# One core: a list scheduler's table counts occupancy and latency of ScalarE and VectorE apart, and the first left operand of the last stage takes another buffer

## Chip, core and metric

The kernel runs on one core of a Trainium2 chip. The metric is the device time of one execution in microseconds (us), lower is better. Engines: TensorE (PE), VectorE (DVE), ScalarE (ACT), GpSimd (POOL) and SyncE (SP), whose queue issues all DMA transfers.

## What is computed

One layer of a hybrid encoder for two groups of rows: a prompt of 1024 frames, and a sample of 32 frames with a cache of 512 keys. The width is 1024, with 8 heads of 64 in each of two attention kinds, all in float32:

```python
qa, ka, va, ga, qb, kb, vb, gb = split(rmsnorm(h, g_pre) @ w_in)       # 1024 -> 8 x 512
oa = band_attention(qa, ka, va, rel_bias)      # own chunk of 64 frames and the 8 before, softmax
ob = stick_breaking(qb, kb, vb)                # w = exp(log_sigmoid(z) + sum of log_sigmoid(-z) of later keys)
y  = concat([oa * silu(ga), ob * silu(gb)]) @ w_out
h  = h + rmsnorm(y, g_post)
h  = h + sigmoid(h @ w_ple_gate) * (p @ w_ple)
```

The outputs are h of both groups and their keys and values.

## The kernel before

**Numbers.** Each float32 product is made of rounded parts: an operand x is split into hi (x rounded) and lo (x less hi), and a product is hi·hi + hi·lo + lo·hi on TensorE. So nearly every operand costs a cast on ScalarE and a subtraction on VectorE or GpSimd before TensorE can use it.

**Stages.** (1) To about 60 us: x is loaded, normalized and transposed. (2) To about 606 us: eight pairs of heads in the order A0, B0, A1, B1, A2, B2, A3, B3, where A is band attention and B stick-breaking. While one pair's attention runs, the projections of the next are computed: mm_q, mm_k, mm_v and mm_g, for each pair in three pieces of 352 columns, of which the name's last number tells (mm_kB2_0 is the first piece of the keys of pair B2). Their banks are two in turn ("mm"). A pair has two heads (SA11 are scores of pair A1, head 1), and a head eight blocks of 128 rows (SB10_3 is block 3 of pair B1, head 0). Scores go through three banks in turn ("S"). Band attention: scores SA, bias and maximum on VectorE (om, statA), exponential on ScalarE with the row's sum (be, sumsA), transposed weights on TensorE (ptwA) or through memory (swapA), split into wTh and wTl, and the product with the values PVA. Stick-breaking: scores SB, exponentials and a scan along the keys (om), weights be, then ptwB or swapB, wTh, wTl and PVB. (3) To 619 us: the products p @ w_ple (ple). (4) To 801 us: the output projection and then the gate, each by a scheme of seven block products in place of eight (P1, P2, P6, P7, P4, P5, P3, in this order). There are four sets of them: two for the output projection (o), two for the gate (g). o0P1 is product P1 of row tile 0; its left operand is A11o0, its right one oB11. P2 has A12o0 and oB21.

**What sets the order.** No order is written out. The kernel is told to a Recorder (L264) in program order; each operation becomes a node with what it must wait for. `Recorder.cost` (L338) gives two numbers for each: `busy`, how long it holds its engine, and `late`, how much later its result is there. `Recorder.order` (L372) plays the nodes through engine by engine: of those ready on the engine that is free first it takes the one with the smallest key (a class, then the program order), and so makes one sequence, by which the instructions then stand on each engine. A user on another engine is ready SEM = 60 ns after the result, one on TensorE another MARGIN = 400 ns later (L432). A DMA counts 1500 ns, its bytes at a rate, and 2000 ns of reserve (L419). Function table loads of ScalarE, which the chip needs when it goes from band attention's exponential to stick-breaking's functions and back, are not in the table; they are put in afterwards. All instructions are emitted at one line of `Recorder.emit`, L450, so the profile tells them apart by their tiles.

**The last stage's first operands.** The right operands oB11, oB21, oT3 and oT2 are split from weights that are staged in eight tiles, woB11_0, woT3_0 and so on to woT3_3 (L1454; each holds a slice of 128 rows of two operands). They go through a ring of two buffers with the tag "ao" in pool fb. The left operands of row tile 0 use the same ring behind them, or a buffer of its own with the same tag in pool fa: `Side.room` (L1539) puts every third one there. The row tile's products come in the order A11, A12, S2, S3, A22, S1, S4, and `taken` counts them. A buffer of the ring is free once the one that had it two tiles before has been read to the end.

Of the kernel before, what the change touches and what calls it, by code (L numbers as in the profile page):

```python
# [8 lines left out]
F32 = mybir.dt.float32  # L9
# [254 lines left out]
class Recorder:  # L264
# [72 lines left out]
    @staticmethod  # L337
    def cost(eng, method, args, kw, writes, reads):  # L338

        out = writes[0] if writes else None  # L340
        n = out.free() if isinstance(out, View) else 1
        psum = any(isinstance(v, (View, Segments)) and v.buf.psum for v in reads)
        if eng == "PE":
            if method == "transpose":
                return (109 if args[1].shape[0] > 64 else 62), 165
            return max(109.0, 2.5 + 0.449 * args[2].free()) * (1 if args[2].buf.dtype == F32R else 4), 165
        if eng == "ACT":
            return (165 if psum else 200) + 0.83 * n + (190 if "accum_out" in kw else 0), 0
        if eng == "DVE":
            if method == "tensor_tensor_scan":  # L350
                return 155 + 2.08 * n, 0
            if method == "tensor_copy" and not psum:
                return 155 + 0.53 * n, 0
            if method == "scalar_tensor_tensor":
                return 210 + 1.04 * n, 0
            return 155 + 1.04 * n + (83 if method == "tensor_tensor_reduce" else 0), 0
        if eng == "POOL":
            if method == "tensor_tensor":
                if n == 1:
                    return 400, 0  # L360
                return 190 + (1.77 if out.buf.dtype == F32 else 2.15) * n, 0
            if method == "tensor_scalar":
                return 255 + 0.86 * n, 0
            return 100 + 0.82 * n, 0
        size, run = 4, 0
        for v in (out, args[1]):
            if isinstance(v, View) and v.buf.pool is not None:
                size, run = 4 * v.shape[0] * v.free(), 4 * v.shape[-1]
        return ISSUE, max(size / DMA_RATE, size / run * (8.5 + 0.0365 * run) / 16)


    def order(self):  # L372
# [10 lines left out]
        free = dict.fromkeys(names, 0.0)  # L383
# [6 lines left out]
        while len(out) < len(self.ops):  # L390
            best = None
            for e in names:
                if now[e]:
                    t = free[e]
                elif soon[e]:
                    t = max(free[e], soon[e][0][0])
                else:
                    continue
                if best is None or t < best[0]:
                    best = (t, e)  # L400
            t, e = best
# [12 lines left out]
            o.at = t  # L414
            if e == "CTL":
                done = t
            elif e == "SP":
                free[e] = t + o.busy
                line = max(line, t + o.busy + DMA_NS) + o.late  # L419
                done = line + DMA_MARGIN  # L420
            else:
                if o.shared:
                    t = max(t, port - (DVE_SET if e == "DVE" else POOL_SET))
                    port = t + o.busy
                free[e] = t + o.busy
# [30 lines left out]
def stream_step(  # L456
# [756 lines left out]
    done = set()  # L1213
# [309 lines left out]
    class Side:  # L1523
# [343 lines left out]
```

## Time and profile before

| | us |
|---|---|
| median of 3 runs | 806.38 (805.48 to 808.88) |
| the profiled execution | 808.3 |
| its span, first to last instruction | 806.5 |
| TensorE busy | 784.5 |
| VectorE busy | 575.5 |
| ScalarE busy | 507.8 |
| GpSimd busy | 436.8 |
| mean granted TensorE clock | 0.996 of full speed |

The profile is of one execution. A row of the timeline gives start, duration, engine, line, operation, out<-in with the tiles' names (numbers left out) and the count of instructions in the row, and in brackets the idle time of the engine just before, with what ended it. A row of waits gives the waiting engine and its tile, what it waited for, and the sum, count and longest in us. A row of windows gives the stretch and, for PE, PEld, DVE, ACT and POOL, busy us and instructions, then the granted clock, the DMA share and GB/s. All times are us from the span's start.

### The profile page before, as it was taken

The page shows a single profiled execution, that of the slowest core. Times are in us where ns is not written, and L with a number is a line of the kernel's source. Part 1 is how long each engine was busy: PE and PEld are TensorE (multiplying, and loading weights), DVE is VectorE, ACT ScalarE, POOL GpSimd, SP SyncE. Part 2 cuts the span into 40 slices and gives each one's busy share as a digit, 9 for nine tenths or more (in the row PEclk, how much of TensorE's full clock was granted, in tenths as well). Part 3 has the DMA queues.
Part 4 walks back from the last instruction along what each step waited for, and adds up shares of the span by engine and source line. Part 5 has one row for each costly group of instructions (what it writes and reads, how often), then busy time and mean ns, then how long its engine had stood idle before and what let it go on. Part 6 is the DMA issues. An engine that isn't in the chain of part 4 may idle for free.

```text
span 806.5 us, 14268 instructions
## 1 busy us (share of the span) xinstructions
PE 784.5 (97%) x4646; PEld 722.4 (90%) x4646; DVE 575.5 (71%) x1007; ACT 507.8 (63%) x1063; POOL 436.8 (54%) x503
## 2 busy tenths in 40 slices
PE   8999999999999999999999999999998999999997
PEld 6899989999889998999999989999996877888786
DVE  6627678886588897778896878766355687586565
ACT  5636675676476655785666685543337867876741
POOL 5613656873556676234660336777541537699523
PEclk9999999999999999999999999999999999999999
DMA  8419987668877749745545667774579767659743
GB/s 275 152 38 276 232 247 243 168 181 237 229 210 228 203 147 272 190 137 152 125 115 159 153 171 231 218 211 151 156 236 329 245 188 231 216 179 343 249 137 131
DMA packets 160971, 161.08 MB, mean 200 GB/s; under 512 B 39153, under 2 KB 120793, under 8 KB 160898
## 3 DMA queue, kind: packets, MB, share of 16 engines
q1 hardware_dynamic: 160898, 160.18, 67.0%
q8 instruction: 37, 0.61, 0.3%
q14 instruction: 36, 0.29, 0.1%
HBM read 99.23 MB, written 52.49 MB: 188 GB/s over the span
## 4 chain that ended last, share of the span: by engine, by line
PE 84%; ACT 5%; POOL 3%; DVE 3%; DMA 2%; issue 2%; SPq 1%; DVEq 0%; ACTq 0%; POOLq 0%
PE mm_gB L450 6%; PE mm_gA L450 6%; PE mm_qA L450 5%; PE mm_kA L450 5%; PE mm_vA L450 5%; PE mm_qB L450 4%; PE mm_kB L450 4%; PE SB L450 4%; PE PVB L450 4%; PE mm_vB L450 3%; PE PVA L450 3%; PE SA L450 3%; PE ptwB L450 3%; PE o0P L450 3%; PE o1P L450 2%; PE g0P L450 2%
## 5 line engine op out<-in xcount | busy, mean ns | idle before, releaser
L450 DVE TENSOR_TENSOR_SCAN om<-om,SB 128x384 f32<-128x384 f32 (+5 forms) x96 | 95.6, 1005 | 12.1 <-ACT om L450 9.8
L450 POOL TENSOR_TENSOR be<-om 128x128 f32<-128x128 f32 (+7 forms) x64 | 77.5, 1216 | 49.4 <-DVE om L450 23.1
L450 ACT ACTIVATE om<-SB 128x384 f32<-128x384 f32 (+5 forms) x96 | 44.9, 494 | 29.9 <-DVE SB L450 17.7
L450 ACT ACTIVATE be<-om,statA 128x640 f32<-128x640 f32 (+3 forms) x64 | 44.5, 696 | 12.1 <-DVE statA L450 6.9
L450 ACT CAST wTh<-ptwB 128x512 fp32r<-128x512 f32 (+3 forms) x64 | 29.4, 482 | 21.1 <-PE ptwB L450 16.2
L450 DVE TENSOR_TENSOR wTl<-be,wTh 128x640 fp32r<-128x640 f32 (+1 forms) x32 | 35.5, 1108 | 7.1 <-ACT wTh L450 6.8
L450 DVE TENSOR_TENSOR wTl<-ptwB,wTh 128x512 fp32r<-128x512 f32 (+3 forms) x64 | 33.5, 545 | 7.7 <-ACT wTh L450 4.6
L450 DVE TENSOR_TENSOR wTl<-ptwA,wTh 128x512 fp32r<-128x512 f32 (+2 forms) x64 | 29.8, 482 | 11.6 <-ACT wTh L450 10.1
L450 PE MATMUL SB<-kdB,LB 128*128 128x384 f32 (+5 forms) x96 | 33.7, 354 | 1.9 <-DVE om L450 1.9
L450 DVE CUSTOM_DVE_ANT_0 om<-SA,biasA 128x320 f32<-128x320 f32 (+3 forms) x64 | 30.0, 483 | 6.2 <-PE SA L450 5.8
L450 PE MATMUL SB<-klB,LB 128*128 128x384 f32 (+5 forms) x96 | 32.9, 347 | 0.0
L450 DVE STREAM_TRANSPOSE om<-be 128x640 f32<-128x640 f32 (+1 forms) x32 | 28.8, 900 | 4.7 <-ACT be L450 2.3
L450 ACT CAST wTh<-ptwA 128x512 fp32r<-128x512 f32 (+2 forms) x64 | 26.1, 424 | 9.0 <-PE ptwA L450 8.2
L450 PE MATMUL SA<-kdA,LA 128*128 128x320 f32 (+2 forms) x96 | 30.0, 322 | 1.3 <-DVE LA L450 0.7
L450 POOL TENSOR_TENSOR sggA<-sggA,oggA 128x352 f32<-128x352 f32 x24 | 23.9, 997 | 13.6 <-DVE sggA L450 10.2
L450 POOL TENSOR_TENSOR oB<-oB,oB 128x256 f32<-128x256 f32 x32 | 24.4, 783 | 12.0 <-DMA oB<-in_w_out_dram 5.8
L450 PE MATMUL SA<-klA,LA 128*128 128x320 f32 (+2 forms) x96 | 29.3, 316 | 0.0
L450 PE MATMUL ptwB<-ident,be 128*128 128x128 f32 x192 | 29.3, 273 | 0.0
L450 ACT CAST wTh<-be 128x640 fp32r<-128x640 f32 (+1 forms) x32 | 24.9, 779 | 6.4 <-DMA be<-swapA 3.8
L450 PE MATMUL ptwA<-ident,be 128*128 128x128 f32 x160 | 26.8, 274 | 2.0 <-ACT be L450 1.3
L450 POOL TENSOR_TENSOR gB<-gB,gB 128x256 f32<-128x256 f32 x32 | 24.3, 783 | 4.7 <-DMA gB<-in_w_ple_gate_dram 4.3
L450 DVE TENSOR_TENSOR SB<-SB,maskb 128x128 f32<-128x128 f32 x64 | 17.6, 290 | 11.3 <-PE SB L450 11.1
(707 smaller groups left out, 2659.7 us busy)
## 6 DMA issues: line engine op xcount, KB each, us to landing
swapA<-om SPq DMA_DIRECT2D x16, 320.0 KB, 2.7
be<-swapA SPq DMA_DIRECT2D x64, 80.0 KB, 3.2
oB<-in_w_out_dram SPq DMA_DIRECT2D x16, 256.0 KB, 4.6
sum_dro<-oB SPq DMA_DIRECT2D x16, 256.0 KB, 3.8
gB<-in_w_ple_gate_dram SPq DMA_DIRECT2D x16, 256.0 KB, 4.2
sum_drg<-gB SPq DMA_DIRECT2D x16, 256.0 KB, 3.0
x<-in_x_prompt_dram SPq DMA_DIRECT2D x16, 256.0 KB, 4.0
h_dr<-h SPq DMA_DIRECT2D x8, 512.0 KB, 3.2
```

Of the source, the lines that this page charges most:

```text
L450: getattr(getattr(tc.nc, o.what[0]), o.what[1])(*args, **kw)
```

## The change

It changes the table of `Recorder.cost`, the moment from which a user on the same engine counts as ready in `Recorder.order`, and one number in `Side.room`. ScalarE's entries move 105 ns from `busy` to `late`, VectorE's 85 (150 for a multiplication with a row sum), and GpSimd's two-input operations get 40 ns of `late`, with 20 less of `busy` (a single column 400 to 535). A user on the same engine counts as ready when the result is there, not when the engine is free; on TensorE this stays as it was.

```diff
         if eng == "ACT":
-            return (165 if psum else 200) + 0.83 * n + (190 if "accum_out" in kw else 0), 0
+            return (60 if psum else 95) + 0.83 * n + (190 if "accum_out" in kw else 0), 105
         if eng == "DVE":
             if method == "tensor_tensor_scan":
-                return 155 + 2.08 * n, 0
+                return 120 + 2.1 * n, 85
...
-            return 155 + 1.04 * n + (83 if method == "tensor_tensor_reduce" else 0), 0
+            if method == "tensor_tensor_reduce":
+                return 90 + 1.04 * n, 150
+            return 70 + 1.04 * n, 85
         if eng == "POOL":
             if method == "tensor_tensor":
                 if n == 1:
-                    return 400, 0
-                return 190 + (1.77 if out.buf.dtype == F32 else 2.15) * n, 0
+                    return 535, 40
+                return 170 + (1.77 if out.buf.dtype == F32 else 2.15) * n, 40
...
             for u in users[id(o)]:
                 if u.eng == e and e != "SP":
-                    r = t if e == "CTL" else free[e]
+                    r = t if e == "CTL" else free[e] if e == "PE" else done
...
             if self.pair == 0:
-                one = Side.taken % 3 == 2
+                one = Side.taken % 3 == 0
```

The rows of all engines change their order. Three places on ScalarE follow. In the rows, numbers behind the underscore at a name's end are of no matter, and the line is L450 before and L452 of the change.

**Pair A1 to pair B1.** Before, from the first stick-breaking exponential (SB10_0) on. be with sumsA11 is the exponential of band attention, om from SB10 the one of stick-breaking:

```order
L450 ACT_TABLE_LOAD
L450 ACTIVATE om_165<-SB10_0_0_2887 128x128
L450 COPY stvB1_2564<-mm_vB1_1_2700 128x352
L450 ACT_TABLE_LOAD
L450 ACTIVATE be_179,sumsA11_1473<-om_165,statA11_7_2775 128x640
L450 COPY otA11_0_2811<-PVA11_0_2995 64x512
L450 CAST wTh_530<-ptwA11_5_0_2988 128x512
L450 CAST wh_kA2_0_2687<-wr_kA2_0_2961 128x512
L450 COPY sumrowA11_2904<-ptsA11_2949 8x128
L450 CAST wh_kA2_1_2693<-wr_kA2_1_2964 128x512
L450 ACT_TABLE_LOAD
L450 ACTIVATE om_165<-SB10_1_0_3005 128x256
```

Of the change, the same place:

```order
L452 ACTIVATE be_179,sumsA11_1435<-om_165,statA11_6_2752 128x640
L452 ACTIVATE be_179,sumsA11_1435<-om_165,statA11_5_2524 128x640
L452 COPY be_179<-PVsA0_2838 32x64 x2
L452 ACTIVATE be_179,sumsA11_1435<-om_165,statA11_7_2753 128x640
L452 CAST wTh_552<-ptwA11_5_0_2942 128x512
L452 ACT_TABLE_LOAD
L452 ACTIVATE om_165<-SB10_0_0_2881 128x128
L452 ACTIVATE om_165<-SB10_1_0_2958 128x256
L452 COPY otA11_0_2814<-PVA11_0_2996 64x512
L452 COPY sumrowA11_2910<-ptsA11_2915 8x128
```

The band exponential with statA11_7 has moved ahead of SB10_0, the copies and casts for the next projections behind SB10_3, and one table load stands where there were three.

**Pair B1 to pair A2.** Before. stvA2 from mm_vA2_2 is the copy that empties a projection's bank; kdA21, LA21, wh_kB2 and wh_qB2 are casts of operands:

```order
L450 CAST kdA21_3847<-stkA2_2922 64x1024
L450 CAST wh_kB2_0_3592<-wr_kB2_0_3786 128x512
L450 CAST LA21_3852<-stqA2_2976 64x1024
L450 CAST wh_kB2_1_3610<-wr_kB2_1_3789 128x512
L450 ACTIVATE om_165<-SB11_7_0_3753 128x512
L450 ACTIVATE om_165<-SB11_7_1_3835 128x512
L450 ACT_TABLE_LOAD
L450 ACTIVATE be_179,sumsA20_2506<-om_165,statA20_0_2777 128x128
L450 COPY stvA2_3343<-mm_vA2_2_3726 128x352
```

Of the change:

```order
L452 CAST wh_kB2_0_3579<-wr_kB2_0_3774 128x512
L452 CAST wh_kB2_1_3585<-wr_kB2_1_3776 128x512
L452 COPY stvA2_3364<-mm_vA2_2_3728 128x352
L452 CAST kdA21_3889<-stkA2_2928 64x1024
L452 CAST LA21_3898<-stqA2_2978 64x1024
L452 ACTIVATE om_165<-SB11_7_1_3876 128x512
L452 ACT_TABLE_LOAD
L452 ACTIVATE be_179,sumsA20_2519<-om_165,statA20_0_2784 128x128
L452 CAST wh_qB2_0_3870<-wr_qB2_0_3777 128x512
```

The copy of mm_vA2_2 has moved ahead of kdA21, LA21, the exponential of SB11_7_1, the table load and the exponential of A20.

**Into the output projection.** Before. A11o0 and A12o0 are the casts of the first left operands, xA11o0 and xA12o0 their copies, uo0 their source, ple the results of stage 3:

```order
L450 COPY xA11o1_7626<-uo1_7540 128x512
L450 CAST whA11o1_7392<-uo1_7540 128x512
L450 CAST oB11_7359<-woB11_3_7598 128x512
L450 CAST oB21_7360<-woB11_3_7598 128x512
L450 COPY ple8_0_7677<-ple8_0_7634 32x512
L450 CAST A11o0_7683<-uo0_6367 128x512
L450 CAST oT3_7362<-woT3_3_7623 128x512
L450 COPY xA12o0_7694<-uo0_6367 128x512
L450 CAST oT2_7361<-woT3_3_7623 128x512
L450 COPY ple8_1_7702<-ple8_1_7645 32x512
L450 CAST S2o0_7531<-s2_0_7668 128x512
L450 CAST A12o0_7715<-uo0_6367 128x512
```

Of the change, first where A11o0 stands now:

```order
L452 CAST oT3_7360<-woT3_1_7441 128x512
L452 CAST oT2_7359<-woT3_1_7441 128x512
L452 ACTIVATE sggB3_2_7472<-mm_gB3_2_7450 128x352
L452 CAST A11o0_7527<-uo0_6402 128x512
L452 CAST php6_7498<-ptp6_7266 128x512
L452 COPY g_post1_7549<-GP_7356 128x512
L452 COPY ple4_0_7281<-ple4_0_6868 128x512
L452 COPY xA11o0_7562<-uo0_6402 128x512
L452 COPY ple4_1_7282<-ple4_1_6877 128x512
L452 CAST oB11_7357<-woB11_2_7515 128x512
```

and, behind these, where A12o0 stands:

```order
L452 COPY ple7_1_7642<-ple7_1_7625 128x512
L452 COPY ple8_0_7664<-ple8_0_7637 32x512
L452 CAST oB11_7357<-woB11_3_7608 128x512
L452 CAST oB21_7358<-woB11_3_7608 128x512
L452 COPY ple8_1_7697<-ple8_1_7648 32x512
L452 CAST A12o0_7702<-uo0_6402 128x512
L452 CAST oT3_7360<-woT3_3_7629 128x512
L452 CAST oT2_7359<-woT3_3_7629 128x512
L452 COPY p1o0_7675<-o0P1_7661 128x512
L452 CAST S3o0_7707<-uo0_6402 128x512
```

A11o0 has moved from behind both casts of woB11_3 to ahead of both casts of woB11_2, and A12o0 now stands just behind those of woB11_3. On TensorE o0P1 with its twelve matmuls is followed by o0P2 with twelve, then o1P1; before, two of o0P1 and two of o1P1 came first, then the other ten, the rest of o1P1 and o0P2.

More of the change, by code (lines that the diff above doesn't have):

```diff
@@ L347, in cost @@
         if eng == "ACT":
-            return (165 if psum else 200) + 0.83 * n + (190 if "accum_out" in kw else 0), 0
+            return (60 if psum else 95) + 0.83 * n + (190 if "accum_out" in kw else 0), 105
         if eng == "DVE":
             if method == "tensor_tensor_scan":
-                return 155 + 2.08 * n, 0
+                return 120 + 2.1 * n, 85
             if method == "tensor_copy" and not psum:
-                return 155 + 0.53 * n, 0
+                return 70 + 0.53 * n, 85
             if method == "scalar_tensor_tensor":
-                return 210 + 1.04 * n, 0
-            return 155 + 1.04 * n + (83 if method == "tensor_tensor_reduce" else 0), 0
+                return 125 + 1.04 * n, 85
+            if method == "tensor_tensor_reduce":
+                return 90 + 1.04 * n, 150
+            return 70 + 1.04 * n, 85
         if eng == "POOL":
```

## The prediction

> **What bounds the kernel now.** I read the busy times first, then the chain of work that ended last, then what TensorE waited for, and only then single places.
>
> ```profile
> PE 784.5 (97%) x4646; PEld 722.4 (90%) x4646; DVE 575.5 (71%) x1007; ACT 507.8 (63%) x1063; POOL 436.8 (54%) x503
> PE 84%; ACT 5%; POOL 3%; DVE 3%; DMA 2%; issue 2%; SPq 1%; DVEq 0%; ACTq 0%; POOLq 0%
> ```
>
> TensorE is busy 784.5 of 806.5 us, and no matmul is added or removed. So the change can win no more than the 22 us in which TensorE stands still, plus matmuls that run slower than they need. ScalarE and VectorE have a third of their time free: a table that makes them look faster gains nothing by itself. It acts only through the order, where TensorE waits. Those waits, with total, count and longest:
>
> ```profile
> PE o0P L450 <- ACT A11o L450: 2.5, 1, 2.5
> PE ptx L450 <- DVE be L450: 2.2, 2, 1.3
> PE SB L450 <- DVE om L450: 1.9, 3, 1.1
> PE mm_kB L450 <- ACT stvA L450: 1.5, 1, 1.5
> PE PVA L450 <- ACT wTh L450: 1.3, 1, 1.3
> PE ptwA L450 <- ACT be L450: 1.3, 1, 1.3
> ...
> PE ptsA L450 <- DVE sumsA L450: 1.0, 2, 0.9
> PE SA L450 <- DVE LA L450: 0.7, 1, 0.7
> ...
> PE SA L450 <- DVE statA L450: 0.6, 1, 0.6
> PE ptwA L450 <- DVE wTl L450: 0.4, 2, 0.2
> ...
> PE ptwA L450 <- ACT ktB L450: 0.3, 1, 0.3
> PE PVsA L450 <- DVE otA L450: 0.2, 1, 0.2
> PE ptkB L450 <- ACT sumrowA L450: 0.2, 1, 0.2
> ```
>
> Three groups: the start (ptx), one wait where the output projection begins (o0P), and 15 small ones in attention. These 15 are the rows from SB to ptkB without o0P and ptx: 1.9+1.5+1.3+1.3+1.0+0.7+0.6+0.4+0.3+0.2+0.2 = 9.4 us, a mean of 0.63 us.
>
> **Does the new table fit the chip?** It says that a 128x512 instruction of ScalarE holds the engine about 100 ns less than it takes, and one of VectorE 85 ns less.
>
> ```profile
> 600.38 0.62 ACT L450 CAST oB<-woB 128x512 fp32r<-128x512 f32 x1
> 609.26 1.14 ACT L450 CAST oB<-woB 128x512 fp32r<-128x512 f32 x2
> 601.13 0.68 DVE L450 TENSOR_TENSOR oB<-woB,oB 128x512 fp32r<-128x512 f32 x1
> 619.91 1.28 DVE L450 TENSOR_TENSOR oB<-woB,oB 128x512 fp32r<-128x512 f32 x2
> ```
>
> One cast takes 0.62, two take 1.14: the second begins 0.52 after the first (1.14−0.62), 100 ns before that one ends. The new entry is 95+0.83·512 = 520 ns held and 105 more until the result is there; the old one was 625 held. For VectorE it is 1.28−0.68 = 0.60 against a new entry of 70+1.04·512 = 602, where the old one held 687. So the planner's idea of both engines was pessimistic by 12 to 16% (85 of 687, 100 of 625) for each queued instruction, and its new one is right. What is planned as ready 0.4 us ahead (MARGIN) will be so more exactly; but what the old table gave away as reserve is used up too. That is why I expect waits to go and others to come.
>
> The Trainium skill speaks against it: "VectorE: DVE Perf Modes", section "The DRAIN you can't avoid", has it that the next VectorE operation does not start until the pipe is empty, by which the old entries would be right. The two VectorE rows above disagree with it (0.60 from start to start, 0.68 for one), so it stays a rival with little weight.
>
> **Part 1, the output projection's first operand (room).** Where TensorE goes from the ple products to o0P:
>
> ```profile
> 621.22 0.62 ACT L450 CAST A11o<-uo 128x512 fp32r<-128x512 f32 x1 [0.32 <-DVE oB L450]
> 621.89 0.99 PE L450 MATMUL o0P<-oB,A11o 128*128 128x512 f32 x2 [2.50 <-ACT A11o L450]
> ```
> ```profile
> 619.00:622.00 3.00, 0.50 (x3) 0.11 (x1) 2.61 (x5) 2.66 (x6) 0.08 (x1) 1.00 1.07 388
> 622.00:626.00 4.00, 4.00 (x11) 3.15 (x12) 4.00 (x4) 2.93 (x6) 2.83 (x2) 0.57 1.14 339
> 626.00:630.00 4.00, 4.00 (x19) 3.26 (x18) 1.44 (x3) 3.12 (x7) 3.68 (x3) 1.00 1.10 333
> ```
> ```profile
> 621.89 0.99 PE o0P L450 x2
> 622.89 0.85 PE o1P L450 x2
> 623.74 3.22 PE o0P L450 x10
> ...
> 629.26 2.74 PE o0P L450 x12
> ```
>
> The cast of A11o0 is held by VectorE's second oB subtraction (the 619.91 row, end 621.19), because its buffer is the ring's that the staged weights use, and the slice woB11_3 must be read first. TensorE waits 2.50 us. The windows (the column after POOL is the granted clock) show the second price: 0.57 in the 4 us behind the wait. The chain gives its size: 14 matmuls from 621.89 to 626.96 (623.74+3.22) take 5.07 us, at the later rate of 2.74/12 = 0.228 each they take 3.2, so **1.9 us** go there; a part is the operands' own lateness, and I take 1.7 for the clock (the 4 us at 0.57 lose 0.43·4 = 1.7).
>
> In the new order the cast of A11o0 stands before the casts of woB11_2 and woB11_3 and needs neither. Then the 12 matmuls of o0P1 can follow the last ple product at 619.3. They use slice 3 only as the tenth, 9·0.228 = 2.1 us later, at 621.4, when both oB halves (end of the 619.91 row at 621.19) are there. What is late next is A12o0, which now takes the ring's place behind woB11_3: cast at 621.2 plus 0.62, so 621.9, where TensorE wants it at 619.3+2.74 = 622.0, and its low half one VectorE step of 0.68 later, 622.5, wanted at its third matmul, 622.5. That is on the edge; I put 0.5 us for a new wait there. **Part 1: −2.5 −1.7 +0.5 = −3.7.** The bounds: −4.2 with no new wait; −1.2 if A12o0 waits as A11o0 did, 2.5, after 12 matmuls and with the clock kept.
>
> By the Trainium skill, "TensorE: Matmul & The Clock Gate", Part 1, half rate follows an idle window of about 3.4 us that runs freely; here 2.50 us of wait sufficed, so a shorter wait may cost it too or not, and by that rule the 1.7 may go or stay.
>
> **Part 2, exponentials of pair A1 against pair B1 (table).** Stick-breaking and band attention use different function tables, which the planner doesn't know.
>
> ```profile
> 234.04 1.28 ACT L450 ACT_TABLE_LOAD   x1
> 235.97 1.28 ACT L450 ACT_TABLE_LOAD   x1
> 240.61 1.28 ACT L450 ACT_TABLE_LOAD   x1
> ```
> ```profile
> 238.48 0.27 PE L450 MATMUL ptsA<-ident,sumsA 128*8 128x128 f32 x1 [0.86 <-DVE sumsA L450]
> 243.19 0.42 PE L450 MATMUL SB<-kdB,LB 128*128 128x320 f32 x1 [1.10 <-DVE om L450]
> ```
>
> SB10_0 goes first, then back for the last exponential of A11, then SB10_1: three loads. In the new order the last exponential (statA11_7) stands ahead of SB10_0 and one load is left. The 0.86 goes, since sumsA needs only that exponential. The 1.10 goes too: SB10_1 follows SB10_0 without a load between them, so the third bank of scores comes free some 4 us sooner. **Part 2: −2.0.** If statA11_7 isn't ready so early, SB10_0 waits behind it and at worst both waits stay: 0. The same flap in pairs A3 and B3 stays in the new order and gets nothing.
>
> The Trainium skill, "ScalarE: Activation LUTs", section "What ACT_TABLE_LOAD costs", counts 1283 ns and a drain of 1380 ns for each switch; here the load takes 1.28, and in the next part's rows the exponential starts 0.01 us behind it, so two loads fewer free 2.6 us of ScalarE, not 5.3.
>
> **Part 3, the copy that frees a projection bank (table).**
>
> ```profile
> 305.94 1.28 ACT L450 ACT_TABLE_LOAD   x1
> 307.23 0.40 ACT L450 ACTIVATE be<-om,statA 128x128 f32<-128x128 f32 x1
> ...
> 307.63 0.43 ACT L450 COPY stvA<-mm_vA 128x352 f32<-128x352 f32 x1
> ```
> ```profile
> 308.12 0.91 PE L450 MATMUL mm_kB<-hnh,wh_kB 128*128 128x352 f32 x4 [1.55 <-ACT stvA L450]
> ```
>
> The copy of mm_vA2_2 sits behind a load and an exponential, and the next bank of mm_kB2 behind the copy. In the new order the copy stands three longer instructions and the load ahead: **−1.5**. I see no reason that it fails; the bound is −1.5 to 0.
>
> **Part 4, everything else that moves.** Attention's rows are reshuffled everywhere, SP's transfers with them. ScalarE and VectorE do the same work, so no busy time changes. A new order by the same rules against a table with less reserve makes new waits. I take as many as go, three, at the mean of the 15: 3·0.63 = **+1.9**; the ends are 0, and 15 more of the same size, +9.4. The remaining 5.9 us of old waits (9.4−3.5) are kept, the bound below is that they go too. The edits for GpSimd (20 ns less held, 40 later; 175 more for a single column) and the readiness of a user on the same engine (85 to 150 ns later) only reorder: no wait of TensorE above is ended by GpSimd, and another ready instruction fills the 85 ns. I put 0 for them; without that cover, 85 ns on a chain of ten VectorE steps is 0.85 once.
>
> **Sum:** −3.7 −2.0 −1.5 +1.9 = **−5.3**. The profiled execution took 808.3 (span 806.5), so its like would take 803.0. It lay 1.9 over the median of 806.38: **801.1**.
>
> **Rivals.**
>
> *New waits eat the gain.* For it: the planner is the same, MARGIN is still 400 ns, and 15 waits came of the last order. With twelve new ones (12·0.63 = 7.6 for the 1.9): +0.4, so 806.8. Against it: the largest ones are named and go.
>
> *Slower: value products come before their weights.* In the new order PVA01_1 stands 23 rows earlier on TensorE (row 300, was 323); PVA20_1 and PVB10_1 also come sooner. Now:
>
> ```profile
> 123.10 0.73 ACT L450 CAST wTh<-be 128x640 fp32r<-128x640 f32 x1
> ...
> 124.70 0.76 PE L450 MATMUL PVA<-wTh,v2A 128*128 128x512 f32 x4
> ```
> ```profile
> be<-swapA SPq DMA_DIRECT2D x64, 80.0 KB, 3.2
> ```
>
> The cast ends at 123.83, 0.87 ahead of its product. 23 rows at TensorE's mean of 784.5/4646 = 0.17 us, or at the 0.23 of a 512-column one, are 3.9 to 5.2 us. If the weights' way (out to memory, 3.2 us back, cast 0.73) doesn't start sooner, TensorE waits 5.2−0.87 = 4.3 there, and by the same reckoning as much at the two others, 13.0 in place of the 1.9: 801.1+11.1 = 812.2; with the clock lost behind each (1.7, as in part 1) 817.3. I take 814. It decides from where the product moves up by 0.9 us more than the transfer that feeds it. Against it: the planner counts the same transfers, and moved the product since it believes them early.
>
> *The change doesn't do what it says.* If instructions do hold VectorE to their ends, ten queued ones are 0.85 late, 0.45 over MARGIN, at perhaps 15 places: +6.8, 807.9. The rows above speak against it.
>
> **Chances.** Forecast (800 to 804 or below) 0.50; new waits eat it 0.32; value products late 0.13; the table wrong 0.05. About 0.5% (4.0 us) is what a measurement of this kernel tells from no change, so faster means under 802.4. My case lies barely over that: of its 0.50 some 0.06 stay within, and 0.03 of the others are faster: faster 0.47. Slower (over 810.4): the value products and 0.03 of the rest, 0.16. Same: 0.37. **Range:** low end: −3.7−0.5−2.0−1.5 and half of the 5.9 that remain, no new waits: −10.7, so 795.7; high end: part 1 at −1.2, parts 2 and 3 at 0, new waits 5.6, between the forecast and the 9.4: +4.4, so 810.8. Left out are most of the late value products and a little below.
>
> **What would show it.** Right: A11o0's cast ends before the last ple product, o0P's wait is under 0.5, and the clock behind it is 1.00; ten table loads in place of twelve, and no waits of ptsA and mm_kB for those causes; other waits in attention sum to about 7.8. Wrong: a wait of PVA or PVB for wTh of over 2 us; a wait of o0P2 for A12o; attention's waits over 12 us; or a longer stretch without TensorE at the start or in the gate stage, where I put nothing.

## The result: no difference that can be measured

| | us |
|---|---|
| before, median of 14 runs | 806.0 (805.1 to 808.88) |
| changed, median of 14 runs | 805.53 (801.88 to 809.23) |
| ratio changed to before | 0.9991, 95% interval 0.9974 to 1.0008 |

Forecast was 801.1. The time lies in the range (795.7 to 810.8), but the gain of 0.65% did not come: the first rival did, "new waits eat the gain", at 806.8. The profiled execution of the changed kernel is the slowest of its 14 (809.23; span 807.4), 3.7 over their median, so a second profile of the same kernel (e1, 804.9, span 803.1, 0.7 under its median) stands beside it.

The page of the changed kernel (busy times, then the chain that ended last):

```profile
PE 788.0 (98%) x4646; PEld 722.3 (89%) x4646; DVE 567.9 (70%) x1007; ACT 504.4 (62%) x1061; POOL 432.1 (54%) x503
PE 72%; DMA 6%; ACT 6%; POOL 5%; DVE 5%; issue 4%; SPq 2%; DVEq 0%; POOLq 0%; ACTq 0%
```

TensorE's share of the last chain fell from 84 to 72%, and that of transfers rose from 2 to 6%. What TensorE waited for:

```profile
PE PVA L452 <- ACT wTh L452: 2.7, 1, 2.7
PE ptx L452 <- DVE be L452: 2.4, 2, 1.3
PE ptwA L452 <- ACT be L452: 1.8, 2, 1.3
PE SB L452 <- DVE om L452: 1.6, 3, 0.9
PE idle L452 <- DVE newh L452: 1.3, 1, 1.3
PE ptkA L452 <- DVE wTl L452: 1.3, 1, 1.3
...
PE o0P L452 <- ACT A12o L452: 0.5, 1, 0.5
```

The rows of o0P for A11o (2.5), of mm_kB (1.5) and of ptsA (1.0) are gone, as forecast. In their place: PVA 2.7 where it was 1.3, and ptkA 1.3, which was not there.

### Where the time went, stretch by stretch

Waits alone do not show a slower clock. So I took from the trace, for each matmul, how much later the next one starts than its shape needs (0.2295 us for 512 columns, 0.161 for 352, 0.109 for a transpose, from undisturbed rows) and summed it by stretches. This **loss** holds waits and half clock both. Span less loss is 773 us in all of these profiles (806.5−33.1 = 773.4; 807.4−34.5 = 772.9; 803.1−30.2 = 772.9; 800.4−27.4 = 773.0). With the same matmuls in each kernel it must come out so: the sum says only that no record is missing, and that two executions differ in time by their loss. e2 has only the changed room, e3 only the changed table.

| stretch, us | before | e2 room | e3 table | changed | changed again, e1 |
|---|---|---|---|---|---|
| 0 to 100 | 8.5 | 8.4 | 7.1 | 7.9 | 7.3 |
| 100 to 200 | 4.6 | 3.8 | 5.6 | 7.9 | 6.9 |
| 200 to 300 | 6.8 | 6.3 | 5.3 | 5.9 | 4.2 |
| 300 to 350 | 2.4 | 2.6 | 3.1 | 2.8 | 2.0 |
| 350 to 600 | 5.0 | 4.8 | 6.1 | 6.2 | 6.0 |
| 600 to 645 | 4.9 | 0.6 | 4.6 | 2.1 | 2.1 |
| 645 to the end | 0.8 | 0.9 | 2.6 | 1.7 | 1.8 |
| sum | 33.1 | 27.4 | 34.3 | 34.5 | 30.2 |

The room's row (600 to 645) moves by 4.3 us between before and e2 and gives nothing back later. The table's rows show what ate it: 200 to 300 wins 1 to 2.6, and 100 to 200, 350 to 600 and the last stage lose more.

Up to 600 us these five columns are two orders and not five: before and e2 have the same rows on every engine up to 606 us, and so have e3, the changed kernel and e1 up to 609 us (the traces' rows, compared by tile and shape). Within such a group only the execution differs. From 100 to 600 us the old rows lose 18.8 and 17.5, the new ones 20.1, 22.8 and 19.1.

The largest place in the changed kernel's profile: ScalarE, then TensorE, then the window with its clock (the column after POOL).

```profile
103.31 0.72 ACT L452 CAST wTh<-be 128x640 fp32r<-128x640 f32 x1 [3.30 <-DMA swapA<-om]
```
```profile
104.08 1.29 PE L452 MATMUL PVA<-wTh,v2A 128*128 128x512 f32 x4 [2.73 <-ACT wTh L452]
```
```profile
100.00:110.00 10.00, 7.27 (x39) 6.69 (x38) 3.56 (x6) 6.60 (x14) 4.39 (x8) 0.83 0.99 268
```

A cast at the head of ScalarE waits 3.30 us for weights that go through memory, with a DMA share of 0.99; PVA waits 2.73, and 0.83 over 10 us is another 1.7 us of clock. What half clock cost at 622 us before, it costs here in this execution. But this wait does not belong to the order: before had 1.3 at this place where e2 has no such row, and of the two other profiles with the new rows e1 has 0.5 and e3 none. The same window in e3, with a DMA share as high:

```profile
100.00:110.00 10.00, 10.00 (x66) 9.37 (x65) 7.42 (x13) 9.41 (x19) 3.59 (x8) 1.00 1.04 266
```

What makes the weights late in one execution and not in another, no run shows.

And the output projection's start in the changed kernel:

```profile
622.54 2.95 PE L452 MATMUL o0P<-oB,A11o 128*128 128x512 f32 x12
626.01 3.29 PE L452 MATMUL o0P<-oB,A12o 128*128 128x512 f32 x12 [0.52 <-ACT A12o L452]
```

o0P1 follows the last ple product without a gap, and the next wait is the one of A12o0, with 0.52 where the prediction put 0.5.

### The profile page after: what moved, and what is told of

Same layout as the page of the kernel before. It is cut to its first block, busy times and chain, and to the rows that moved or that the text cites. A ratio compares the mean times of both kernels' runs of the same rounds, so it can differ in the third digit from the quotient of the medians.

```text
span 807.4 us, 14271 instructions
## 1 busy us (share of the span) xinstructions
PE 788.0 (98%) x4646; PEld 722.3 (89%) x4646; DVE 567.9 (70%) x1007; ACT 504.4 (62%) x1061; POOL 432.1 (54%) x503
## 4 chain that ended last, share of the span: by engine, by line
PE 72%; DMA 6%; ACT 6%; POOL 5%; DVE 5%; issue 4%; SPq 2%; DVEq 0%; POOLq 0%; ACTq 0%
PE mm_gA L452 6%; PE mm_gB L452 6%; PE mm_kA L452 5%; PE mm_qA L452 5%; PE mm_qB L452 4%; PE SB L452 3%; PE mm_vA L452 3%; PE PVB L452 3%; PE mm_kB L452 3%; PE PVA L452 3%; PE mm_vB L452 3%; PE SA L452 2%; PE o1P L452 2%; PE g2P L452 2%; PE g3P L452 2%
## 5 line engine op out<-in xcount | busy, mean ns | idle before, releaser
L452 POOL TENSOR_TENSOR be<-om 128x128 f32<-128x128 f32 (+7 forms) x64 | 75.4, 1184 | 64.8 <-DVE om L452 29.0
L452 DVE TENSOR_TENSOR_SCAN om<-om,SB 128x384 f32<-128x384 f32 (+5 forms) x96 | 94.9, 1001 | 9.1 <-ACT om L452 7.4
L452 ACT ACTIVATE om<-SB 128x384 f32<-128x384 f32 (+5 forms) x96 | 44.4, 493 | 36.0 <-DVE SB L452 26.9
L452 ACT ACTIVATE be<-om,statA 128x640 f32<-128x640 f32 (+3 forms) x64 | 44.4, 694 | 18.2 <-DVE statA L452 11.0
L452 DVE TENSOR_TENSOR wTl<-be,wTh 128x640 fp32r<-128x640 f32 (+1 forms) x32 | 37.6, 1175 | 10.3 <-ACT wTh L452 8.8
L452 ACT CAST wTh<-ptwB 128x512 fp32r<-128x512 f32 (+3 forms) x64 | 29.5, 481 | 19.6 <-PE ptwB L452 15.4
L452 DVE TENSOR_TENSOR wTl<-ptwB,wTh 128x512 fp32r<-128x512 f32 (+3 forms) x64 | 33.7, 545 | 10.3 <-ACT wTh L452 7.8
L452 DVE TENSOR_TENSOR wTl<-ptwA,wTh 128x512 fp32r<-128x512 f32 (+2 forms) x64 | 29.8, 483 | 15.7 <-ACT wTh L452 12.5
L452 POOL TENSOR_TENSOR oB<-oB,oB 128x256 f32<-128x256 f32 x32 | 27.7, 882 | 18.6 <-DMA oB<-in_w_out_dram 10.5
L452 DVE STREAM_TRANSPOSE om<-be 128x640 f32<-128x640 f32 (+1 forms) x32 | 28.9, 904 | 9.8 <-POOL be L452 4.9
L452 PE MATMUL SB<-kdB,LB 128*128 128x384 f32 (+5 forms) x96 | 34.0, 357 | 1.6 <-DVE om L452 1.6
L452 DVE CUSTOM_DVE_ANT_0 om<-SA,biasA 128x320 f32<-128x320 f32 (+3 forms) x64 | 29.5, 482 | 7.6 <-PE SA L452 4.4
L452 ACT CAST wTh<-ptwA 128x512 fp32r<-128x512 f32 (+2 forms) x64 | 26.2, 426 | 13.3 <-PE ptwA L452 7.5
L452 PE MATMUL SB<-klB,LB 128*128 128x384 f32 (+5 forms) x96 | 32.9, 345 | 0.0
L452 PE MATMUL SA<-kdA,LA 128*128 128x320 f32 (+2 forms) x96 | 30.2, 325 | 0.7 <-DVE LA L452 0.4
L452 POOL TENSOR_TENSOR sggA<-sggA,oggA 128x352 f32<-128x352 f32 x24 | 23.8, 991 | 11.2 <-DVE sggA L452 10.8
L452 PE MATMUL SA<-klA,LA 128*128 128x320 f32 (+2 forms) x96 | 29.6, 320 | 0.0
L452 ACT CAST wTh<-be 128x640 fp32r<-128x640 f32 (+1 forms) x32 | 25.0, 782 | 6.4 <-DMA swapA<-om 3.3
L452 PE MATMUL ptwB<-ident,be 128*128 128x128 f32 x192 | 28.7, 273 | 0.0
L452 PE MATMUL ptwA<-ident,be 128*128 128x128 f32 x160 | 26.3, 276 | 2.0 <-ACT be L452 1.8
L452 DVE TENSOR_TENSOR SB<-SB,maskb 128x128 f32<-128x128 f32 x64 | 17.3, 287 | 13.5 <-PE SB L452 13.1
L452 POOL TENSOR_TENSOR klA<-stkA,kdA 64x1024 fp32r<-64x1024 f32 x8 | 20.7, 2587 | 8.2 <-ACT kdA L452 7.7
```

What stands on the lines that cost most here:

```text
L452: getattr(getattr(tc.nc, o.what[0]), o.what[1])(*args, **kw)
```

## The experiments

Two theories. **Theory 1:** an order is a draw. Its waits at places that nobody named differ from order to order by more than the named ones are worth, whatever the table. **Theory 2:** the new table leaves too little reserve, and that brings the new waits. The runs of before beside them had medians of 806.7 to 807.1.

### The changed kernel again, and its two parts (e1 to e3)

e1 has no edit.

> The changed kernel once more, unchanged, for a second profile, since the first one (809.23 us) was the slowest of its 14 executions. Theory 1 (the new order brings fixed new waits: PVA00_1 at about 104 us, ptkA1 at 151, SB11_4 at 288): these three rows are there again with 2.7, 1.3 and about 1, whatever the time. Rival (the wait of PVA00_1, which hangs on a transfer through memory, and the half clock behind it differ from execution to execution and make the spread of 802 to 809): in a faster execution the PVA00_1 wait is under 1.5 us and no half clock stands behind it, ptkA1 and SB11_4 stay. Time 805.5, ratio 0.997 to 1.001.

805.57 (804.24 to 808.77), ratio 0.9996 [0.998, 1.0012]. ptkA1 is there again (1.4), PVA00_1 has only 0.5, SB11_4 nothing, but ptwA01_5_4 waits at 116 us instead:

```profile
PE PVA L452 <- ACT wTh L452: 0.5, 1, 0.5
```
```profile
113.71 0.73 ACT L452 CAST wTh<-be 128x640 fp32r<-128x640 f32 x1 [2.36 <-DMA be<-swapA]
...
116.07 0.97 PE L452 MATMUL ptwA<-ident,be 128*128 128x128 f32 x5 [1.87 <-DVE wTl L452]
```

It is the same kind of cause 12 us later, a cast at the head of ScalarE that waits for weights from memory. So neither expectation held whole: the waits for transfers between 100 and 118 us wander between executions, but there are some in each (loss from 100 to 150 us without ptkA1: 5.8 in the first profile, 4.6 in this one, 3.5 in e3; 3.2 before, 2.5 in e2). ptkA1 is fixed (1.3 in e3 too).

```diff
-                one = Side.taken % 3 == 2
+                one = Side.taken % 3 == 0
```

> Only the room of the first left operand is changed, the table is that of before. Theory 1 (the room's gain is real and is eaten by the table's new waits): the o0P wait for A11o of 2.5 us goes, a wait of about 0.5 for A12o comes, the time falls by about 3 us to 803, ratio 0.996. Rival (the output projection is limited by its transfers, and the time won at its start is lost again before 715 us): ratio 0.999 to 1.001.

803.19 (801.49 to 809.89), ratio 0.9979 [0.9956, 1.0002]. Two windows of it around the start of the output projection:

```profile
600.00:620.00 20.00, 20.00 (x97) 16.32 (x97) 10.84 (x18) 16.13 (x31) 5.45 (x4) 1.00 0.92 310
620.00:640.00 20.00, 20.00 (x89) 16.37 (x88) 14.15 (x21) 17.65 (x35) 10.60 (x8) 1.00 0.93 291
```

TensorE is busy without a break at full clock. The trace shows the gain where it was expected, and none is lost after it; the interval of the time just reaches no change, since this kernel's executions lie apart, and their mean clocks with them (below).

The other half, the table and the readiness with the old room:

```diff
-                one = Side.taken % 3 == 0
+                one = Side.taken % 3 == 2
```

> Only the table and the readiness are changed, the room is that of before. Theory 1: attention as in the changed kernel (no ptsA, SB10_4 and mm_kB2 waits of before, but PVA00_1, ptkA1 and SB11_4), a wait of o0P for A11o of about 2.5 stays; attention loses as much as it wins and the whole is at 807 to 809, ratio 1.001 to 1.004. Rival (the table wins 3 us, and the changed room costs them): about 803, ratio 0.996.

809.7 (807.2 to 812.99), ratio 1.0043 [1.0027, 1.0059]: theory 1's side, and a little above its numbers.

```profile
PE o0P L452 <- ACT A11o L452: 2.3, 1, 2.3
...
PE ptwA L452 <- DVE wTl L452: 1.4, 1, 1.4
...
PE ptkA L452 <- DVE wTl L452: 1.3, 1, 1.3
```
```profile
620.00:640.00 20.00, 18.58 (x74) 15.04 (x75) 15.65 (x24) 18.58 (x37) 11.72 (x9) 0.91 0.88 286
```

The room's wait and its half clock (0.91 over 20 us, 1.8 us) are back, ptkA1, SB11_4 (0.9) and the wait at 115 us stay; PVA00_1, which was expected, does not wait here. So the change is the sum of a room that wins some 3.6 us (806.8 to 803.2) and a table that loses most of it again (2.4 on top of e2, 2.9 on top of before).

### Is it the table, its reserve, or the draw? (e4 to e12)

The changed kernel with the readiness line put back:

```diff
-                    r = t if e == "CTL" else free[e] if e == "PE" else done
+                    r = t if e == "CTL" else free[e]
```

> The changed kernel with the one line of the readiness of users on the same engine put back (they count as ready when the engine is free). ScalarE's order then has the three table loads from A1 to B1 again, twelve in all. If the line made the gain of the flap: waits of ptsA or SB10 of about 2 us at 235 to 245 come back, time 806 to 808. If any other draw of the order is worth as much: within 2 us of the changed kernel, with other waits at other places.

819.34 (818.31 to 820.35), ratio 1.0165 [1.0145, 1.0185], so neither: 14 us more, with waits everywhere (loss 45.2; 200 to 250 us 7.3, 350 to 400 us 3.9 and 625 to 645 us 4.7). What the next runs show forbids reading a price of the line out of it.

e5 to e8 change nothing but MARGIN, by 10 ns, with either table and the new room:

```diff
-MARGIN = 400
+MARGIN = 390   # e5, e7; 410 in e6, e8
```

> The room is the changed one, the table that of before, and MARGIN 390 in place of 400 ns. Ten ns are worth nothing by themselves, but they break ties and give another order (16 table loads by it, where 400 gives 12). Theory 1 (an order is a draw, whose waits in attention sum to some 3 us more or less whatever the table): 3 us or more away from the 803.2 of MARGIN 400, with other waits at other places; more likely slower, for four loads more, about 807. Theory 2 (the table's accuracy is what counts): within 1 us of 803.2.

> As the run before with MARGIN 410 (12 table loads). Theory 1: anywhere from 800 to 809, not the waits of MARGIN 400. Theory 2: within 1 us of 803.2, the flap at 235 to 245 us and the mm_kB2 wait at 307 there again.

> The changed kernel with MARGIN 390 (14 table loads by the order). Theory 1: 801 to 812, differing from the 805.6 of MARGIN 400 by some 3 us. Theory 2 (the new table by itself leaves too little reserve and costs 2 to 3 us against the old): 805 to 807, above both runs with the old table.

> The changed kernel with MARGIN 410 (10 table loads by the order, as with 400). Theory 1: 801 to 812, and the mean of the three new-table orders is within the spread of the three old-table ones. Theory 2: 805 to 807, above both runs with the old table.

And by 100 ns or more:

```diff
-MARGIN = 400
+MARGIN = 500   # e9 new table, e12 old table; e10: 600, new table; e11: 300, old table
```

> The changed kernel with MARGIN 500: users on TensorE are planned 100 ns later, about what the new table took off each queued instruction of ScalarE and VectorE. Theory 2 (the new table is tight; its neighbours at 390 and 410 took 819 and 821 since the reserve was used up): 803 to 810, attention from 100 to 600 us loses 14 to 18 us as with the old table, not 27. Theory 1 (an order is a draw and nothing else): no better than 390 and 410 on the average, 806 to 822.

> As the run before with MARGIN 600. Theory 2: 803 to 810 again, the loss in attention not over 18 us. Theory 1: 806 to 822, without any relation to the run with 500.

> The old table with the changed room and MARGIN 300, so a reserve that is 100 ns smaller. Theory 2: it looks like the new table at 400 and its neighbours, 812 to 821, with a loss in attention of 22 us and more. Theory 1: 803 to 815, as the three old-table runs before (803, 810, 812).

> The old table with the changed room and MARGIN 500, so a reserve that is 100 ns larger. Theory 2: at or under the old-table runs at 390 to 410, 800 to 808. Theory 1: 803 to 815.

Medians, all with the new room, and the ratio to before:

| MARGIN | old table | new table |
|---|---|---|
| 300 | 813.5 (1.0084 [1.0058, 1.0109]) | |
| 390 | 809.9 (1.0037 [1.0011, 1.0062]) | 818.8 (1.0150 [1.0124, 1.0176]) |
| 400 | 803.2 (0.9979 [0.9956, 1.0002]) | 805.6 (0.9996 [0.9980, 1.0012]) |
| 410 | 811.8 (1.0075 [1.0052, 1.0098]) | 820.8 (1.0165 [1.0136, 1.0194]) |
| 500 | 819.6 (1.0165 [1.0132, 1.0198]) | 807.7 (1.0022 [0.9999, 1.0046]) |
| 600 | | 821.0 (1.0174 [1.0145, 1.0202]) |

Ten ns of margin, which are worth nothing by themselves, move the time by 7 to 15 us. The number of table loads does not order the times either: ten loads took 805.6 and 820.8, twelve 803.2 and 821.0. More reserve does not help the new table (807.7, but 821.0), and spoils the old one (819.6, where theory 2 had 800 to 808): **theory 2 falls** as it was put. Its times for e9 and e11 came true, but those were theory 1's too; of the loss from 100 to 600 us it was right in e11 (28) and wrong in e9 (24) and e10 (33.5), where it had at most 18. Of five orders each, the old table's took 811.6 on the average and the new one's 814.8, inside a spread of 16 us in either, and the new one is slower at 390, 400 and 410 but faster at 500: on these ten orders neither table is shown to be the better, and a difference of a few us is not excluded. **Theory 1 stands**, and the draws lie further apart than its own ranges: e6, e7, e8 and e12 took more than it allowed. 400 gives the best of five with both tables; why, no run shows. The longest single waits of the four orders that are 10 ns away from 400:

```profile
PE ptwA L450 <- ACT be L450: 3.2, 1, 3.2
```
```profile
PE mm_kB L450 <- ACT stvA L450: 1.8, 1, 1.8
```
```profile
PE mm_vB L452 <- ACT wh_vB L452: 2.8, 1, 2.8
```
```profile
PE PVA L452 <- DVE sumsA L452: 3.7, 1, 3.7
```

They are e5, e6, e7 and e8: four orders, four places, and none is the place of the changed kernel's longest; e6's is that of part 3. A long wait often brings clock too: the profiled spans of e7 and e8 have a mean of 0.990 and 0.989, but those of e5 and e6 0.998.

### Single edits of a fixed order (e13 to e18)

To price one place, the order itself was kept, and single instructions were moved in it; the traces' rows of all engines are otherwise the same. "later(a, b)" puts a behind b with what depends on it, "sooner(a, b)" puts a ahead of b.

```diff
         ops = self.order()
+        self.later(ops, exp_SB10_0, exp_A11_7)    # on e2's order
```

> The order of e2 (old table, changed room) with one edit: the exponential of SB10_0 stands behind the band exponential with statA11_7, as in the new order. TensorE, VectorE, GpSimd and SyncE have word for word the same rows as e2, ScalarE has two table loads less (ten). If the price of part 2 of the prediction is right: the waits of ptsA (0.9) and SB10_4 (1.1) at 237 to 243 us go, the loss of TensorE between 200 and 250 us falls from 5.0 to about 3.0, the time by 2 to 801. Rival (SB10_0 being later makes a wait of its own): the loss there stays at 4 to 5 and the time at 803.

804.52 (801.86 to 811.54), ratio 0.9972 [0.9941, 1.0003]; against e2's 0.9979 no gain. Both named waits are gone with two of three loads, and another is there, on VectorE and then TensorE:

```profile
238.08 0.48 DVE L470 TENSOR_TENSOR_SCAN om<-om,SB 128x128 f32<-128x128 f32 x1 [2.71 <-ACT om L470]
```
```profile
238.61 0.50 PE L470 MATMUL SB<-kdB,LB 128*128 128x512 f32 x1 [1.87 <-DVE om L470]
```

The scan of SB10_0 stands at the head of VectorE, waits 2.71 us for the later exponential, and the score banks with it. Loss from 200 to 250 us: 7.0, in e2 5.0; 1.7 of the 7.0 is half clock behind this wait (granted clock 0.50 from 240 to 243 us), which e2 does not have there. The rival was right: the price is handed on. In the changed kernel this stretch does win (3.8 and 3.0). There VectorE's and TensorE's rows moved along; that this makes the difference is argued, no run tried it.

```diff
+        self.sooner(ops, copy_mm_vA2_2, exp_A20_0)    # on e2's order
```

> The order of e2 with one other edit: the copy of mm_vA2_2 stands ahead of the table load and A20's first exponential, all else word for word as e2. If the price of part 3 is right: the wait of mm_kB2 for stvA (1.6) at 307 us goes, the loss between 300 and 350 us falls from 2.6 to about 1.0, the time by 1.5 to 801.7. Rival (the wait is only handed on to A20's exponential and its transposes): a wait of ptwA20 of 1 us or more comes at 308 to 315.

802.08 (800.8 to 804.22), ratio 0.9944 [0.9927, 0.9962]: the first kernel here whose interval lies wholly under before; with that of e2 it overlaps. Of the 1.6 us of mm_kB2, 0.5 remain, and these for another engine:

```profile
PE mm_kB L470 <- POOL wl_kB L470: 0.5, 1, 0.5
```

Loss from 300 to 350 us: 1.6, in e2 2.6. Part 3 was worth 1.0 in its stretch, not 1.5.

```diff
+        self.later(ops, cast_wThA01_1_from_beA01_4, exp_SB00_4_0)    # on the changed kernel's order
+        self.later(ops, sub_wTlA01_1_from_beA01_4, sub_wTlA01_1_from_ptwA01_5_0)
```

> The changed kernel's order with one edit at 111 to 114 us: the cast of wThA01_1 from beA01_4, which stands at the head of ScalarE waiting for its transfer from memory, and its subtraction stand two casts later, behind those from ptwA01_5_0. All else word for word as in the changed kernel. Theory (the new waits from 100 to 118 us come of casts planned before their transfers land): the wait of ptwA01_5_4 (1.9 in e1) goes, the loss from 100 to 150 us falls from 5 to 6.2 to 2.5 to 4, the time by 2 to 3 to 803. Rival (it is the transfers' own lateness, and TensorE waits for them a little later): a wait of PVA01_1 or ptwA01_7 takes its place, the loss stays at 5 to 6.

806.33 (804.0 to 808.44), ratio 0.9991 [0.9976, 1.0007]. The rival was right: loss from 100 to 150 us 5.9, in e1 6.2, and the wait is now at another transpose.

```profile
116.18 0.26 ACT L473 COPY sumrowA<-ptsA 8x128 f32<-8x128 f32 x1 [1.90 <-DMA o_dr<-otA]
```
```profile
116.48 0.66 PE L473 MATMUL ptwA<-ident,be 128*128 128x128 f32 x4 [1.89 <-ACT sumrowA L473]
```

The next instruction on ScalarE that needs a transfer to have ended, here the store of a buffer that it writes, holds TensorE for the same 1.9.

```diff
+        self.later(ops, sub_wTlB00_1_from_beB00_4, sub_wTlB00_1_from_ptwB00_5_4)    # on the changed kernel's order
```

> The changed kernel's order with one edit at 145 us: VectorE's subtraction wTlB00_1 from beB00_4, with both inputs in the on-chip buffer, which takes 2.9 us beside GpSimd's klA10, stands behind the two subtractions from ptwB00_5, which read from the accumulators. All else word for word. Theory (VectorE's two-buffer operations stand still while GpSimd's run, and the new order puts one ahead of work that TensorE waits for): the wait of ptkA1 (1.3 to 1.4 at 150 us) goes, the time by 1.4 to 804. Rival (VectorE is late there whatever stands first): the wait stays, or moves to PVB00_1, with 1 us or more.

803.47 (801.99 to 807.48), ratio 0.9958 [0.9941, 0.9974]; e1 had 0.9996. VectorE, GpSimd and TensorE in e1:

```profile
145.52 2.91 DVE L452 TENSOR_TENSOR wTl<-be,wTh 128x640 fp32r<-128x640 f32 x1 [0.66 <-ACT wTh L452]
```
```profile
145.37 2.39 POOL L452 TENSOR_TENSOR klA<-stkA,kdA 64x1024 fp32r<-64x1024 f32 x1
```
```profile
149.78 0.27 PE L452 MATMUL ptkA<-ident,stkA 128*32 128x128 f32 x1 [1.39 <-DVE wTl L452]
```

and in e16, where the same subtraction comes third and takes 0.82, and ptkA1 waits for nothing:

```profile
148.30 0.82 DVE L472 TENSOR_TENSOR wTl<-be,wTh 128x640 fp32r<-128x640 f32 x1
```
```profile
148.84 0.27 PE L472 MATMUL ptkA<-ident,stkA 128*32 128x128 f32 x1
```

This new wait is explained and removable. The time fell by about 2 us (e1 805.57), of which the wait itself is 1.4.

```diff
+        self.later(ops, load_wr_vA1_0, load_beA01_4)    # on SyncE, with the edits of e15 and e16
+        self.later(ops, load_oB111, load_beA01_6)
```

> The changed kernel's order with the edits of e15 and e16 and two more on SyncE at 106 to 113 us: the load oB111 of the background weight sums, which stands at the queue's head waiting for its buffer, and the load wr_vA1_0 are issued behind the weights that come back from memory (be from swapA), so the store of otA00_1, on whose buffer the copy sumrowA01 waits, goes out sooner. TensorE's and GpSimd's rows are word for word the same. Theory (at 100 to 118 us the order makes ScalarE and the queue wait at their heads for transfers): the ptwA01 wait of 1.9 falls under 0.8, the loss from 100 to 150 us from 5.9 to 2 to 3.5, and with the ptkA1 wait gone the time is 801 to 802.5. Rival (GpSimd then waits for oB111 and the scores behind it, or another wait takes its place): a wait of SB00 of 1 us or more, loss 4 to 6, time 803.5 as e16.

806.06 (804.32 to 809.05), ratio 0.9992 [0.998, 1.0004]: the ptwA01 wait falls to 0.6 as expected, yet the time rises by 2.6 over e16. As the rival had it, another wait takes its place, 13 us later:

```profile
129.37 0.47 PE L476 MATMUL SB<-kdB,LB 128*128 128x448 f32 x1 [1.85 <-DVE om L476]
```

That GpSimd gets oB111 later, and the scores wait for that, is argued from GpSimd's order, not shown: no run took it away. The profiled execution is the slowest of its 12 (809.05). Its loss from 100 to 150 us is 8.3, over both expectations: besides this wait, PVA00_1 waits 1.85 again, and 1.7 is half clock from 130 to 133 us.

```diff
+        self.later(ops, exp_A31_7, exp_A31_5)    # on e14's order
```

> The order of e14 (old table, changed room, the copy edit) with one more edit on ScalarE at 469 us: of three band exponentials in a row the one with statA31_5, for which TensorE's transposes wait 1.3 us, goes ahead of the one with statA31_7. Else word for word as e14. If single waits can be taken out of a fixed order at their price: the ptwA31_5 wait falls to 0.5, the loss from 450 to 500 us from 2.8 to 2.0, the time to 801.3, ratio 0.992 to 0.996. Rival (handed on as in e13): ptwA31_7 or PVA31 waits 0.8 more, time 802.

802.23 (801.3 to 802.81), ratio 0.9942 [0.9927, 0.9958], the same as e14.

```profile
PE ptwA L471 <- ACT be L471: 0.5, 1, 0.5
PE PVA L471 <- ACT be L471: 0.5, 1, 0.5
```

The wait of 1.3 is now 0.5, and PVA31 waits 0.5 that were not there; the loss from 450 to 500 us stays (2.7, was 2.8). Handed on again.

## Why the prediction was wrong, by its steps

- **What bounds the kernel: right.** The matmuls are the same in every order profiled here, and only TensorE's loss moves.
- **Part 1, the room, −3.7: right.** e2 alone: 4.3 less loss at 600 to 645 us, 806.8 to 803.2. The changed kernel: 2.8 less. The half clock behind the wait was there to be won (e3: 0.91 over 20 us with the wait, e2: 1.00 without). The 0.5 for A12o0 was 0.52 in the changed kernel, and a further 1.0 us of slower matmuls behind it, at full clock, was not forecast; e2 has neither.
- **Part 2, the exponentials, −2.0: right in size, wrong in reason.** The stretch from 200 to 250 us won 1.8 to 2.6. But e13 made on ScalarE the move that the prediction argued from, took out the same two loads and both waits, and won nothing: SB10_0 then waits behind statA11_7, which the prediction had only as its bound of 0. The gain belongs to the rearrangement as a whole, and that it had the forecast size is luck.
- **Part 3, the copy, −1.5: right, a third too large.** e14: −1.0, since the bank then waits 0.5 for GpSimd's wl_kB.
- **Part 4, +1.9: the step that failed.** "I take as many as go, three, at the mean of the 15." In the profiled execution of the changed kernel, ten places lose more than they do in e2: PVA00_1 2.9, ptkA1 1.5, SB11_4 1.1, ptwA11_5 and o0P2 0.7 each, PVA10_0 0.6, SA21_1, PVB11, g0P6 and SB10_3 between 0.4 and 0.5 each (losses, which run a tenth or two over the waits), 9.2 together, and 1.7 of clock at 104 us. That is the upper end that the prediction gave for the term, and it took a value near its lower one. In e1 such places sum to 6.6 (ptwA01_5_4 2.0 for most of PVA00_1, no SB11_4). Two of these numbers are not the term's: o0P2 was counted in part 1, and PVA00_1 with its clock is that execution's, not the order's.
- **What the new places cost in place of 1.9** is read better from all five profiles. From 100 to 600 us, where parts 2 to 4 lie, the new rows lose 2.5 more than the old ones on the average (20.7 and 18.2), where −1.6 was forecast (−2.0−1.5+1.9). If parts 2 and 3 brought their 3.5, the new places cost about 6, not 1.9; that is an estimate, since executions of one order differ by 3.7 here. With −2.8 for part 1, 0.9 more in the last stage, where the prediction put nothing, and 1.0 less up to 100 us, the change comes to about −0.4; the medians differ by 0.5.
- **Its own signs.** Those of being right came: A11o0's cast ends at 610 us, long before the last ple product, the clock behind it is 1.00, ten loads, no waits of ptsA and mm_kB, and attention's waits sum to 8.8 (7.8 forecast). Of those of being wrong came PVA's wait for wTh of over 2 us (2.7) and o0P2's for A12o. So the list of waits hardly tells the failure; the loss, with half clock and slower matmuls in it, does.
- **The argument behind part 4 failed too:** "a table with less reserve makes new waits" was theory 2, and the MARGIN series does not bear it out. That the table fits the chip better is true of its rows; on these orders it bought nothing.
- **The rivals.** The first came true. The slower one named a mechanism that is seen, a value product that waits for its weights' transfer, but at places that show no such wait in either profile of the changed kernel; the place is PVA00_1 at 104 us, where one of 1.3 stood before and where the executions of one order differ.
- **Luck.** That the time lies in the stated range is the draw's doing: the same change with MARGIN 390 or 410 took 818.8 and 820.8, over its high end.
- **Open:** what the readiness line is worth (e4 changed it and took 14 us more, but a different draw does as much), and which of the new rows makes most of the other small waits: only ptkA1 was traced to one (e16).

## What to carry to other kernels

Where a list scheduler writes the order of a kernel that is 97% busy, a change to its table is first of all another draw: price the named places if you will, but take the spread of the draws (move a margin by 2.5% and run it) as the width of what can come, before believing a gain below it. What survives is a change that leaves most of the order alone: a buffer that removes a wait (e2, whose rows change only from 606 us on) or one moved instruction (e14, e16). And even then look at what stands next at the head of the queues, since four of the six such edits here only handed the wait on.

## What the runs showed of the hardware

- **The granted clock falls to half for 3.4 us at a time, behind waits of TensorE.** Narrow windows show 0.50 (before from 622.5 to 625.5 us, the changed kernel from 105 to 107). In all twenty profiles such a stretch within the work lasts 3.4 us, or twice that, so it costs 1.7 us of matmuls, or 3.4. Behind each of the 15 waits of 2.0 us or more one begins, from 1.4 us before the wait's end to 1.2 after it (once 3.0 after). Of ten waits of 1.8 to 2.0 us, five have one, four have none, and one falls into a stretch that runs already. Most profiles also have one at their end, behind the last matmul, where it costs nothing but lowers the mean.
- **Executions of one program differ in mean clock, and in time with it.** In e2, seven executions with 0.999 or 1.000 took 801.8 to 803.5, four with 0.994 to 0.997 took 807.7 to 809.9, and one with 0.998 took 801.5. The clock is not all of it: 0.003 to 0.006 of 800 us is 2.4 to 4.8 us, and they took 4 to 8 more. That waits which come and go, with half clock behind them, make the rest is argued: no profile shows one of the slower executions. One profile can mislead here, as the first one of the changed kernel did in part.
- **A subtraction of VectorE with both inputs in the on-chip buffer stands still while GpSimd's runs.** In e1 it ended 0.67 us after GpSimd's (145.37+2.39 = 147.76; 145.52+2.91 = 148.43), which is nearly its own length (0.82 in e16). Of e1's 24 subtractions of this shape, the eight that begin 0.39 us or more before the end of a GpSimd instruction all end 0.67 to 0.69 us after it, and the other 16 take 0.80 to 0.83; in the profile of before, two began 1.4 and 2.0 us ahead of such an end and still took 0.8. The Trainium skill, "SBUF — State Buffer", in its table of terms, has the two engines share a port pair that one holds for a whole instruction while the other is blocked; these rows agree.
- **Two function table loads fewer (2.6 us of ScalarE) did not shorten the kernel** (e13), with ScalarE busy for 63% of the span.
